# Cross attention's queries as seven block products per pair of heads, and the pooling mixer's bias and scale rows loaded ahead of its first sums

## The chip, the cores and the metric

The kernel runs on one core of one Trainium2 chip. Its engines, with the names that the profile uses: TensorE (PE for matmuls, PEld for loading their stationary operand), VectorE (DVE), ScalarE (ACT), GpSimd (POOL) and SyncE (SP), which here only issues transfers. The metric is the device time of one execution in microseconds, the median of several runs. Before the change it is 1936.6 us, from 1935.6 to 1938.74 over three runs.

## The reference

Two layers of a decoder trunk over 512 tokens of width 1024, in float32. Layer 0 mixes tokens by differential attention, layer 1 by a causal pooling mixer; both layers then attend to 256 memory tokens with 4 heads of 256, and a half-step SwiGLU feed-forward stands at either end of a layer.

```python
for i in range(DEPTH):
    x = layer_norm(a * x + 0.5 * swiglu_ffn(x, ffn_w_in[i, 0], ffn_w_out[i, 0]), ...)
    h = diff_attention(...) if i == 0 else pool_mixer(x, pool_w[j], pool_b[j], pool_scale[j])
    x = layer_norm(a * x + h, ...)
    x = layer_norm(a * x + memory_cross_attention(x, mem, xa_wq[i], xa_wkv[i], xa_wo[i]), ...)
    x = layer_norm(a * x + 0.5 * swiglu_ffn(x, ffn_w_in[i, 1], ffn_w_out[i, 1]), ...)

def pool_mixer(x, w_grp, b_grp, scale):
    ...
    pooled = jnp.stack(pooled, axis=2) - xg
    y = jnp.einsum('bsgc,gcd->bsgd', pooled, w_grp) + b_grp
    return y.reshape(B, S, D) * scale

def memory_cross_attention(x, mem, wq, wkv, wo):
    q = (x @ wq).reshape(B, S, XA_HEADS, XA_HEAD_DIM)
    k, v = jnp.split(mem @ wkv, 2, axis=-1)
    s = jnp.einsum('bshd,bmhd->bhsm', q, k) * (XA_HEAD_DIM ** -0.5)
    p = jax.nn.softmax(s, axis=-1)
    o = jnp.einsum('bhsm,bmhd->bshd', p, v).reshape(B, S, D_MODEL)
    return o @ wo
```

## The kernel before

**Numbers.** Every float32 operand of a matmul is split into a high part (ScalarE casts it to fp32r) and a low part (VectorE subtracts the high one from it): `split`, lines 120 and 121, or `split_scaled`, lines 125 and 126. Each product is then three matmuls, high by high, high by low and low by high (`mm3`, lines 205 to 207). So every weight tile costs one ScalarE cast and one VectorE subtraction before PE can use it.

**Stages.** The token rows lie in four tiles X, 128 tokens each. Each stage ends in sums that are added to X, followed token tile by token tile by the layer norm (`ln_token`, lines 366 to 380, with one small operation of GpSimd for the root), and the next stage's operands are the transposes of X (`turn`, tiles pt), split into xh and xl. The feed-forward already multiplies by seven block products instead of eight (`up`, `second_factors`, `seven`, `down`): both matrices are cut in two by two blocks, sums of blocks are made, and seven products of them are combined. It makes the sums of weight blocks by loading a further block onto the tile in place: a transfer from GpSimd's queue with an addition (line 666). `factors` 0 to 3 are the four blocks of the transposed X (0 and 1 for tokens 0 to 255, upper and lower half of the features; 2 and 3 for the other tokens, 3 being a difference), 4 to 6 sums of them.

**Cross attention.** `xa_main` is a generator that issues matmuls in program order, and `weave` lets a second generator, `xa_side`, take a step each time the first has issued a given number of estimated nanoseconds (2500 here). The main one makes, head by head, keys and values of the memory (`xa_k`, `xa_v`, banks pk and pv) and the head's queries (lines 1441 to 1452, banks xq): one transfer of 1 MB of `xa_wq`, two tiles of weights split, 16 groups of three matmuls of 512 tokens, and a scaled split of each of the two banks. The side steps of a head are its scores and softmax (banks xs, tiles p), the transposes of p, and the products with the values (banks xo), whose splits oT feed `to_tokens`, which multiplies by `xa_wo` and adds to X. In layer 1 the keys and values of heads 0 and 1 and the keys of head 2 are made ahead (`early_kv`), while the pooling mixer runs as its side.

**Pooling mixer.** X is split untransposed; for each of eight column blocks of 128, banks pp collect matmuls with a band matrix, and the block is split into a tile `pooled`. At block 2 (line 1261) `pool_weights` is issued: ScalarE scales the bias rows, GpSimd multiplies them by the scale rows, VectorE multiplies the mixer's weights pw by the scale rows (line 1239), and GpSimd adds the bias to X (line 1243). pw, the rows (tiles ps) and the norm's gains are loaded by `load_more`, which stands inside the first head's keys.

**Queues and tiles.** Each tile tag has a number of buffers; an instruction that writes a new tile waits until the buffer's last user is done, and a stage's tiles lie where those of the stage before lay. Every engine works through its instructions in an order that is fixed when the program is built; SP's transfers are issued in order, so one that waits for a buffer holds those behind it. Before, the stages around the change have five buffers each for the high and low weights (wh, wl) and two of 8 KB per partition for raw weights.

## Time and profile before

| | us |
|---|---|
| median of three runs | 1936.6 |
| the profiled execution | 1932.35 |
| its span, first to last instruction | 1930.6 |
| PE busy in it | 1902.1 |
| DVE busy in it | 1566.3 |
| ACT busy in it | 1022.2 |
| POOL busy in it | 315.0 |
| layer 0's cross attention, about | 591 to 736 |
| layer 1's pooling mixer with early keys and values, about | 1407 to 1464 |
| layer 1's cross attention, about | 1464 to 1597 |

All rows are of one profiled execution. A row of a timeline gives the start, the duration (of a merged group, to its end), engine, line and operation, what it writes and reads, and in square brackets how long the engine stood idle before it and what ended that. A row that groups gives count, total busy time, the mean of one in nanoseconds, and the idle time before. A row of stretches gives the busy time of each engine in it, and the granted clock of PE as a share of full speed. Matmuls are pipelined, so the time that one of them takes on PE is read from start to start and not from its duration.

### The profile page before, as it was taken

Reading aid. Unit: us, or ns where it says so; the run is one execution under the profiler, and the core shown is the slowest. Engines: PE = TensorE matmul, PEld = TensorE weight load, DVE = VectorE, ACT = ScalarE, POOL = GpSimd, SP = SyncE. Lnnn points to the kernel's source line nnn. Section 1 sums busy time; section 2 is a strip of 40 time slices with the busy share of each in tenths; the row PEclk is TensorE's granted clock in tenths of the full one; section 3 lists DMA queues with packets and bytes.
Section 4 is the critical chain, followed back from the end, with each engine's and each line's share of the span. In section 5 each row is a group of like instructions: output and inputs, shape, how many; then the busy total and the mean of one; then the engine's idle time right before and its main releaser. Section 6 shows DMA issues by size and latency. Waiting matters only on the chain.

```text
span 1930.6 us, 32520 instructions
## 1 busy us (share of the span) xinstructions
PE 1902.1 (99%) x13114; PEld 1740.5 (90%) x13114; DVE 1566.3 (81%) x2200; ACT 1022.2 (53%) x1580; POOL 315.0 (16%) x276
## 2 busy tenths in 40 slices
PE   8999999999999999999999999999999999999998
PEld 8999998888778888999998999999889889999997
DVE  7888889888867557888888988898887568988886
ACT  6555454567655435655554655455445436555553
POOL 2112121111210001211210321112040012111210
PEclk9999999999999999999999999999999999999999
DMA  9978772322134316977686587778244356867861
GB/s 239 220 169 182 175 138 77 90 80 74 48 117 142 110 66 186 186 175 164 139 194 179 104 179 168 177 162 185 89 153 134 115 140 120 181 158 170 183 133 56
DMA packets 246743, 277.96 MB, mean 144 GB/s; under 512 B 8256, under 2 KB 212544, under 8 KB 246592
## 3 DMA queue, kind: packets, MB, share of 16 engines
q0 software_dynamic: 92928, 92.29, 31.1%
q1 hardware_dynamic: 153664, 183.59, 29.2%
q8 instruction: 103, 1.69, 0.3%
q14 instruction: 48, 0.39, 0.1%
HBM read 273.75 MB, written 2.10 MB: 143 GB/s over the span
## 4 chain that ended last, share of the span: by engine, by line
PE 80%; DVE 12%; ACT 3%; DMA 2%; issue 2%; POOL 1%; SPq 1%; DVEq 0%; ACTq 0%; POOLq 0%
PE x L205 7%; PE x L206 7%; PE x L207 7%; PE z L206 4%; PE z L205 4%; PE z L207 4%; PE ps L205 4%; PE ps L207 4%; PE ps L206 4%; PE px L205 2%; PE px L207 2%; PE px L206 2%; DVE wl L121 2%; PE y L207 2%; PE x L681 2%
## 5 line engine op out<-in xcount | busy, mean ns | idle before, releaser
L666 POOL DMA_DIRECT2D ra<-in_ffn_w_in_dram x132 | 170.3, 1309 | 993.5 <-DVE wl L121 815.2
L120 ACT CAST wh<-ra 128x1024 fp32r<-128x1024 f32 x184 | 193.7, 1053 | 218.9 <-PE x L206 67.5
L121 DVE TENSOR_TENSOR wl<-ra,wh 128x1024 fp32r<-128x1024 f32 x184 | 223.8, 1220 | 73.0 <-ACT wh L120 72.5
L120 ACT CAST wh<-rc 128x1024 fp32r<-128x1024 f32 x136 | 143.1, 1053 | 118.6 <-PE x L206 43.1
L205 PE MATMUL x<-xe,wh 128*128 128x256 f32 x704 | 195.0, 277 | 0.0
L206 PE MATMUL x<-xe,wh 128*128 128x256 f32 x704 | 194.8, 277 | 0.0
L207 PE MATMUL x<-xe,wl 128*128 128x256 f32 x704 | 194.8, 277 | 0.0
L121 DVE TENSOR_TENSOR wl<-rc,wh 128x1024 fp32r<-128x1024 f32 x136 | 164.6, 1219 | 28.4 <-ACT wh L120 28.1
L120 ACT CAST wh<-b 128x1024 fp32r<-128x1024 f32 x112 | 117.8, 1052 | 131.3 <-PE x L206 67.7
L121 DVE TENSOR_TENSOR wl<-b,wh 128x1024 fp32r<-128x1024 f32 x112 | 136.7, 1220 | 40.2 <-ACT wh L120 40.2
L205 PE MATMUL x<-xh,wh 128*128 128x256 f32 x544 | 151.1, 278 | 0.0
L206 PE MATMUL x<-xl,wh 128*128 128x256 f32 x544 | 150.6, 277 | 0.0
L207 PE MATMUL x<-xh,wl 128*128 128x256 f32 x544 | 150.6, 277 | 0.0
L206 PEld LDWEIGHTS x<-xe,wh 128*128 128x128 f32 x704 | 132.5, 188 | 1.4
L205 PEld LDWEIGHTS x<-xe,wh 128*128 128x128 f32 x704 | 132.1, 188 | 1.3
L207 PEld LDWEIGHTS x<-xe,wl 128*128 128x128 f32 x704 | 132.2, 188 | 0.0
L121 DVE TENSOR_TENSOR wl<-raw,wh 128x1024 fp32r<-128x1024 f32 x64 | 81.8, 1285 | 38.8 <-ACT wh L120 38.2
L206 PEld LDWEIGHTS x<-xl,wh 128*128 128x128 f32 x544 | 102.5, 188 | 0.7
L205 PEld LDWEIGHTS x<-xh,wh 128*128 128x128 f32 x544 | 102.1, 188 | 0.7
L207 PEld LDWEIGHTS x<-xh,wl 128*128 128x128 f32 x544 | 102.1, 188 | 0.0
L207 PE MATMUL y<-xh,wl 128*128 128x256 f32 x352 | 98.4, 280 | 1.2
L206 PE MATMUL z<-xl,wh 128*128 128x256 f32 x352 | 97.5, 277 | 0.7 <-DVE xl L121 0.7
(429 smaller groups left out, 6291.6 us busy)
## 6 DMA issues: line engine op xcount, KB each, us to landing
ra<-in_ffn_w_in_dram POOLq DMA_DIRECT2D x132, 512.0 KB, 6.7
rc<-in_ffn_w_in_dram SPq DMA_DIRECT2D x88, 512.0 KB, 5.8
b<-in_ffn_w_out_dram SPq DMA_DIRECT2D x76, 512.0 KB, 4.8
ra<-in_ffn_w_in_dram SPq DMA_DIRECT2D x44, 512.0 KB, 5.4
rc<-in_ffn_w_in_dram POOLq DMA_DIRECT2D x44, 512.0 KB, 6.7
raw<-in_xa_wkv_dram SPq DMA_DIRECT2D x16, 1024.0 KB, 5.4
raw<-in_da_w_qkv_dram SPq DMA_DIRECT2D x16, 512.0 KB, 5.2
raw<-in_xa_wq_dram SPq DMA_DIRECT2D x8, 1024.0 KB, 4.9
```

What stands on the lines that cost most here:

```text
L120: self.nc.scalar.copy(hi, src),
L121: self.nc.vector.tensor_sub(lo, src, hi.bitcast(F32)),
L205: mm(out, w[0], x[0], start=start, stop=False, skip_group_check=again)
L206: mm(out, w[0], x[1], start=False, stop=False, skip_group_check=again)
L207: self.last_mm = mm(out, w[1], x[0], start=False, stop=stop, skip_group_check=again)
L666: nc.gpsimd.dma_start(t, source(*block), accum_op=ALU.add)
L681: self.last_mm = nc.tensor.matmul(ps[:, j], v[i][:, k, j * P : (j + 1) * P], x[l][:, k], start=n == i == l == 0, stop=n == 7 and i == 1, s ...
```

## The change

**Queries.** Two heads form a pair; the query weights of a pair are cut into four blocks of 512 rows by 256 columns (one column block for each head) and the transposed X into four of 512 features by 256 tokens. `xa_queries` makes seven products of 24 matmuls each. The weights' sums are made as in the feed-forward: one raw tile takes block (1, 1) and then three additions in place, another takes (2, 2) and one addition, each issued on GpSimd's queue behind the split of what stood in the tile. `xa_factors` makes the factors from the transposes of token tiles 2 and 3 (its parts are issued at each `s` of `XA_ORDER`), so `turn` serves only tiles 0 and 1. `XA_ORDER` writes out, for each layer, in what order the main work is issued: `q` and `r` are a product of the first and second pair, a digit is a part of that head's keys and values, `Q` and `R` hand the pair's heads to the side work.

**Buffers.** Raw weights come in pieces of 4 KB per partition, with five buffers in layer 0 and four in layer 1, and `to_tokens` takes its weights in the same pieces; wh and wl have four buffers instead of five. The side's step is 2100 instead of 2500.

**Pooling mixer.** The rows of scale and bias are no longer loaded in `load_more` but in `pool_bias`, which is issued right behind the first head's raw keys and values, into tiles p of the stage, and which also holds their two multiplications. `pool_weights` is issued at block 1 instead of 2. Behind the last token tile's sums no `turn` is issued.

```diff
+XA_ORDER = ("0000s00ss" "qq1q11qq1q11qQ" "r222r2r22rr3rrR33333", "qsqs2qsq2sq3qqQ" "r2r3rr33rrrR33")
...
+            ns = ns or 0
...
+    def raw_quarter(self, w, r0, c0, width):
+        raw = self.raw_tile((4 * 256 // width, width))
+        rows = w[r0 : r0 + P * 4 * 256 // width, c0 : c0 + width]
+        self.last_load = self.nc.sync.dma_start(raw, rows.rearrange("(k p) n -> p k n", p=P))
+        return raw
+    def raw_keys(self, w, h):
+        return [self.raw_quarter(w, 0, h * 256 + j * P, P) for j in range(2)]
+    def raw_values(self, w, h):
+        return [self.raw_quarter(w, r, D + h * 256, 256) for r in (0, S)]
...
-        for k in range(0, kn, 4):
-            n = min(4, kn - k)
-            raw = self.raw_tile((4, S))
+        got, n = [], self.raw_rows
+        for k in range(0, kn, n):
+            raw = self.raw_tile((n, S))
             r0 = (k0 + k) * P
             self.nc.sync.dma_start(
-                raw[:, :n], w[r0 : r0 + n * P, c0 : c0 + S].rearrange("(k p) n -> p k n", p=P)
+                raw, w[r0 : r0 + n * P, c0 : c0 + S].rearrange("(k p) n -> p k n", p=P)
             )
             if homes:
-                got += [home() for home in homes]
-                for j, t in enumerate(got):
+                got += [home() for home in homes[k : k + n]]
+                for j, t in enumerate(got[k:]):
                     self.split(t[0], t[1], raw[:, j])
...
-        if self.ln_next == "ffn":
+        if self.ln_next != "da":
...
+    def pool_bias(self):
+        nc = self.nc
         rows, self.pool_rows = self.a["pool_b"].rearrange("l g c -> l (g c)"), []
         for half in range(2):
             c = slice(half * S, (half + 1) * S)
-            sc, bs = self.tmp("ps"), self.tmp("ps")
+            sc, bs = self.tmp("p"), self.tmp("p")
             nc.sync.dma_start(sc, self.a["pool_scale"][:, c].to_broadcast([P, S]))
             nc.sync.dma_start(bs, rows[:, c].to_broadcast([P, S]))
+            nc.scalar.mul(bs, bs, 1.0 / ALPHA)
+            nc.gpsimd.tensor_tensor(bs, bs, sc, ALU.mult)
             self.pool_rows.append((sc, bs))
 
     def pool_weights(self):
 
         nc = self.nc
         for half, (sc, bs) in enumerate(self.pool_rows):
-            nc.scalar.mul(bs, bs, 1.0 / ALPHA)
-            nc.gpsimd.tensor_tensor(bs, bs, sc, ALU.mult)
...
-            if c == 2:
+            if c == 1:
...
-            self.turn_late()
+            if t < NT - 1:
+                self.turn_late()
...
-    def xa_kv(self, w, h):
-        kt = self.keys.pop(0) if self.keys else (yield from self.xa_k(w, h))
-        return kt, (yield from self.xa_v(w, h))
-    def xa_k(self, w, h, raw=None, then=None, turn=True):
-        rk = raw or self.raw_cols(w, h * 256)
+    def xa_kv(self, w, h, turn=None):
+        kt = self.keys.pop(0) if self.keys else None
+        if not kt:
+            kt = yield from self.xa_k(w, h, turn=turn)
+            yield None
+        self.kv.append((kt, (yield from self.xa_v(w, h))))
+    def xa_k(self, w, h, raw=None, then=None, turn=None):
+        rk = raw or self.raw_keys(w, h)
         ps = self.mm("pk").rearrange("p (c n) -> p c n", c=2)
         for j in range(2):
+            wk = self.hl([P, KC, P])
             with self.after(self.x_split if raw and not then else ()):
-                wk = self.cols(rk, j)
+                self.split_weights(wk[0], wk[1], rk[j])
             if then and j == 1:
                 then()
             for k in range(KC):
                 yield self.mm3(
                     ps[:, j], (wk[0][:, k], wk[1][:, k]), self.memT[k], k == 0, k == KC - 1
                 )
+            yield None
         kt = self.kv_tiles((P, 2, MEM))
         if turn:
-            self.turn_late()
+            turn()
         self.split(kt[0], kt[1], ps)
...
-            o = self.pair("oT")
-            self.split(o[0], o[1], po)
-            self.oT.append(o)
+            if c == 0:
+                o = self.pair("oT" if len(self.oT) < 4 else "xe", (P, 2, S))
+            self.split(o[0][:, c], o[1][:, c], po)
+            self.oT.append((o[0][:, c], o[1][:, c]))
...
+    def xa_factors(self):
+        nc, F, H = self.nc, self.factors, 2 * P
+        a11, a12, a21, s1 = (self.tmp("oT", (P, 4, H)) for i in range(4))
+        def part(i, x, o=slice(0, H)):
+            self.split(F[i][0][:, :, o], F[i][1][:, :, o], x)
+        for t in (2, 3):
+            o = slice(t % 2 * P, (t % 2 + 1) * P)
+            pts = []
+            for half in range(2):
+                pt = self.aux("pt", ("py", "yz")[half]).rearrange("p (c n) -> p c n", c=4)
+                c0 = half * S
+                with self.behind():
+                    self.transpose4(pt, [self.X[t][:, c0 + j * P : c0 + (j + 1) * P] for j in range(4)])
+                pts.append(pt)
+            nc.scalar.copy(a21[:, :, o], pts[0])
+            nc.vector.tensor_tensor(s1[:, :, o], pts[1], a21[:, :, o], ALU.subtract)
+            part(3, s1[:, :, o], o)
+            part(2, pts[1], o)
+            yield
+        for r, (hi, lo) in zip((a11, a12), F):
+            nc.vector.tensor_tensor(r, hi.bitcast(F32), lo.bitcast(F32), ALU.add)
+        s2, s4, s3 = s1, a12, a21
+        nc.vector.scalar_tensor_tensor(s2, s1, -1.0, a11, ALU.mult, ALU.subtract)
+        nc.vector.scalar_tensor_tensor(s4, s2, -1.0, a12, ALU.mult, ALU.subtract)
+        part(6, s4)
+        yield
+        part(4, s2)
+        nc.vector.tensor_tensor(s3, a11, a21, ALU.subtract)
+        part(5, s3)
+        yield
+    def xa_queries(self, w, h, q):
+        nc, H = self.nc, 2 * P
+        def source(row, col):
+            c0 = (h + col - 1) * H
+            return w[(row - 1) * S : row * S, c0 : c0 + H].rearrange("(k p) n -> p k n", p=P)
+        def load(*block):
+            t = self.raw_tile((4, H))
+            nc.sync.dma_start(t, source(*block))
+            return t
+        def more(t, *block):
+            nc.gpsimd.dma_start(t, source(*block), accum_op=ALU.add)
+        def operand(raw):
+            v = self.hl([P, 4, H])
+            self.split_weights(v[0], v[1], raw)
+            return v
+        def product(ps, v, a, start=False):
+            x = self.factors[a]
+            for j in range(2):
+                o = slice(j * P, (j + 1) * P)
+                for k in range(4):
+                    yield self.mm3(
+                        ps[:, j], (v[0][:, k, o], v[1][:, k, o]), (x[0][:, k], x[1][:, k]),
+                        start and j == k == 0, j == 1 and k == 3, True,
+                    )
+        bank = lambda t: t.rearrange("p (j n) -> p j n", j=2)
+        halves = slice(0, H), slice(H, S)
+        scale = (D // XA_H) ** -0.5
+        def done(i, half, src, by):
+            hi, lo = (t[:, :, halves[half]] for t in q[i])
+            self.split_scaled(hi, lo, src, by)
+        ra = load(1, 1)
+        x = bank(self.aux("x", "px"))
+        v = operand(ra)
+        more(ra, 1, 2)
+        rc = load(2, 1)
+        yield from product(x, v, 0, True)
+        p1 = self.tmp("p", (P, 2, H))
+        nc.scalar.copy(p1, x)
+        yield None
+        y = bank(self.aux("y", "yz"))
+        v = operand(rc)
+        yield from product(y, v, 1, True)
+        nc.vector.tensor_tensor(p1, y, p1, ALU.add)
+        q[0] = self.pair("q", (P, 2, S))
+        done(0, 0, p1, scale)
+        yield None
+        z = bank(self.aux("z", "yz"))
+        v = operand(ra)
+        rd = load(2, 2)
+        more(ra, 2, 2)
+        yield from product(z, v, 3, True)
+        p5 = self.tmp("p", (P, 2, H))
+        nc.scalar.copy(p5, z)
+        yield None
+        v = operand(rd)
+        more(rd, 1, 2)
+        yield from product(z, v, 6)
+        yield None
+        v = operand(ra)
+        more(ra, 2, 1)
+        yield from product(x, v, 4)
+        u2 = self.tmp("p", (P, 2, H))
+        q[1] = self.pair("q", (P, 2, S))
+        nc.scalar.copy(u2, x)
+        nc.vector.tensor_tensor(u2, z, u2, ALU.add)
+        done(1, 0, u2, -scale)
+        yield None
+        yield from product(x, operand(rd), 5)
+        nc.vector.tensor_tensor(p5, x, p5, ALU.add)
+        done(1, 1, p5, -scale)
+        yield None
+        yield from product(x, operand(ra), 2)
+        done(0, 1, x, scale)
+        yield None
+    def part(self, units):
+        for ns in units:
+            if ns is None:
+                return
+            yield ns
...
     def xa_main(self, layer):
         wq, wkv = self.a["xa_wq"][layer], self.a["xa_wkv"][layer]
-        early = len(self.kv)
-        for h in range(XA_H):
-            if h >= len(self.kv):
-                self.kv.append((yield from self.xa_kv(wkv, h)))
-            kt, v = self.kv[h]
-            raw = self.raw_cols(wq, h * 256)
-            qs = []
-            ws = [self.cols(raw, c) for c in range(2)]
-            ps = [self.mm("xq") for c in range(2)]
-            for p in ((0, 2 * P), (2 * P, S)) if self.late else ((0, S),):
-                for c in range(2):
-                    yield from self.project(ps[c], ws[c], (p,))
-                    self.turn_late(max(len(self.late) - 1, 0) if c == 0 else 0)
-            for c in range(2):
-                q = self.pair("q")
-                self.split_scaled(q[0], q[1], ps[c], (D // XA_H) ** -0.5)
-                qs.append(q)
-            self.heads.append((self.clock, (qs, kt, v)))
-            if 0 < early and h + early < XA_H:
-                self.kv.append((yield from self.xa_kv(wkv, h + early)))
+        self.late, second = [], self.xa_factors()
+        qs = [[None] * 2 for n in range(2)]
+        works = {n: self.xa_queries(wq, 2 * i, qs[i]) for i, n in enumerate("qr")}
+        works.update((str(h), self.xa_kv(wkv, h)) for h in range(1, XA_H))
+        works["0"] = self.xa_kv(wkv, 0, lambda: next(second))
+        for n in XA_ORDER[layer]:
+            if n == "s":
+                next(second)
+            elif n in "QR":
+                i = "QR".index(n)
+                for j in range(2):
+                    q = [(qs[i][j][0][:, c], qs[i][j][1][:, c]) for c in range(2)]
+                    self.heads.append((self.clock, 2 * i + j, q))
+            else:
+                yield from self.part(works[n])
         yield from self.to_tokens(self.oT, self.a["xa_wo"][layer], 0, 4, True, False, ALPHA)
 
     def xa_side(self):
         for h in range(XA_H):
-            while h >= len(self.heads) or self.clock < self.heads[h][0] + 3000:
+            while h >= min(len(self.heads), len(self.kv)) or self.clock < self.heads[h][0] + 3000:
                 yield WAIT
-            yield from self.xa_head(*self.heads[h][1])
+            yield from self.xa_head(self.heads[h][2], *self.kv[h])
...
-        bufs = dict(q=8, oT=10, gb=2)
+        bufs = dict(xe=6, q=4, oT=4)
+        self.raw_rows = 2
         if layer == 0:
             self.kv, self.keys = [], []
             mem = self.side_pool("mem")
-            with self.other_pools():
+            with self.stage_pools(4, dict(raw=5), ("wh", "wl", "raw", "kv")):
                 self.stage["mem"] = mem
-                with self.phase_pool(("gb", "gb"), "p", pT=6, p=4, kv=8, _x=0, **bufs):
-                    self.kvp = self.phase["kv"]
+                with self.phase_pool(("xe", "xe"), "p", p=4, pT=4, _x=0, **bufs):
+                    self.kvp = self.stage["kv"]
                     with self.tc.high_priority():
                         self.load_memory("p")
                     self.xa(layer, ln)
             self.close_side()
         else:
-            with self.later, self.phase_pool(("gb", "gb"), "p", _x=0, pT=6, p=4, **bufs):
+            with self.later, self.phase_pool(("xe", "xe"), "p", _x=0, pT=4, p=4, **bufs):
                 self.xa(layer, ln)
 
     def xa(self, layer, ln):
-        self.heads, self.oT = [], []
-        self.weave(self.xa_main(layer), self.xa_side(), 2500)
+        self.heads, self.oT, self.factors = [], [], self.factor_tiles()
+        self.weave(self.xa_main(layer), self.xa_side(), 2100)
...
-            self.later.enter_context(self.other_pools(("wh", "wl", "mem", "raw")))
+            self.later.enter_context(self.stage_pools(4, dict(raw=4), ("wh", "wl", "mem", "p", "raw")))
             self.to_w(self.later)
             self.kvp = self.later.enter_context(self.pool("kv"))
-            bufs = dict(pw=1, ps=4, gb=2, _x=0, pooled=16, sq=1)
+            bufs = dict(p=4, pw=1, gb=2, _x=0, pooled=16, sq=1)
             with self.phase_pool(("gb", "gb"), "sq", **bufs):
                 side = self.pool_mixer(layer, ln)
                 with self.tc.high_priority():
                     self.load_memory()
                 w = self.a["xa_wkv"][layer]
-                raws = [self.raw_cols(w, c) for c in (0, D)]
+                raws = [self.raw_keys(w, 0), self.raw_values(w, 0)]
+                self.pool_bias()
```

24 lines of the change are left out of this document (13 added, 11 removed).

## The prediction

> **What bounds the kernel now.** I read the page first, then busy time by stretch for both cross-attention stages and one stretch of feed-forward, then the timeline of each engine through the pooling mixer.
>
> ```profile
> span 1930.6 us, 32520 instructions
> PE 1902.1 (99%) x13114; PEld 1740.5 (90%) x13114; DVE 1566.3 (81%) x2200; ACT 1022.2 (53%) x1580; POOL 315.0 (16%) x276
> 591.00:736.00 145.00, 144.80 (x895) 128.27 (x894) 82.61 (x129) 59.58 (x113) 1.08 (x1) 1.00 0.37 119
> 1464.00:1597.00 133.00, 132.53 (x772) 115.12 (x769) 80.69 (x136) 56.48 (x112) 5.72 (x6) 1.00 0.45 135
> 800.00:1000.00 200.00, 199.71 (x1496) 188.81 (x1496) 176.59 (x223) 109.43 (x134) 36.04 (x28) 1.00 0.77 173
> ```
>
> The three stretches are layer 0's cross attention, layer 1's, and a stretch of feed-forward; the columns are busy time and instructions of PE, PEld, DVE, ACT and POOL, then the clock, the DMA share and GB/s. PE is the bound. In the two cross-attention stages it sits idle 0.2 and 0.5 us, while DVE is busy 82.6 of 145 us and 80.7 of 133. So a matmul taken out there shortens the run by its own spacing, as long as nothing else becomes late. The feed-forward row is what the new scheme looks like when it runs well: the same seven-product pattern, DVE at 176.6 of 200 us, PE idle 0.3.
>
> The one large hole that the change touches is in the pooling mixer:
>
> ```profile
> 1381.31 28.37 SPq L233 DMA_DIRECT2D raw<-in_xa_wkv_dram  x3
> 1412.65 8.90 DMA ps<-in_pool_b_dram
> 1421.57 0.63 ACT L1234 ACTIVATE ps<-ps 128x512 f32<-128x512 f32 x1 [1.89 <-DMA ps<-in_pool_b_dram]
> 1419.77 1.43 POOL L1235 TENSOR_TENSOR ps<-ps 128x512 f32<-128x512 f32 x1 [5.55 <-ACT ps L1234]
> 1421.28 3.77 POOL L1243 TENSOR_TENSOR X<-X,ps 128x512 f32<-128x512 f32 x3
> 1425.00 1.73 POOL L1235 TENSOR_TENSOR ps<-ps 128x512 f32<-128x512 f32 x1
> 1426.70 9.58 POOL L1243 TENSOR_TENSOR X<-X,ps 128x512 f32<-128x512 f32 x5
> 1422.71 0.69 DVE L121 TENSOR_TENSOR pooled<-pp,pooled 128x512 fp32r<-128x512 f32 x1 [2.66 <-ACT pooled L120]
> 1424.52 6.17 DVE L1239 TENSOR_TENSOR pw<-pw,ps 128x512 f32<-128x512 f32 x4
> 1437.42 0.58 PE L206 MATMUL ps<-wl,pooled 128*128 128x256 f32 x1 [3.11 <-DVE wl L121]
> 1437.79 0.41 PE L207 MATMUL ps<-wh,pooled 128*128 128x256 f32 x1
> ...
> 1440.57 0.41 PE L205 MATMUL pv<-wh,mem4h 128*128 128x256 f32 x1
> 1437.00:1439.00 2.00, 1.58 (x7) 1.58 (x8) 2.00 (x3) 0.00 (x0) 0.00 (x0) 0.61 1.07 376
> 1439.00:1441.00 2.00, 2.00 (x12) 2.00 (x11) 2.00 (x4) 0.00 (x0) 0.00 (x0) 0.53 0.16 51
> ```
>
> The last bias row is issued at 1412.65 and takes 8.9 us. ACT waits for it (1421.57), and behind ACT's multiplication stands its cast of the first pooled block, so DVE idles 2.66 us until 1422.71. DVE then needs 6.17 us for four weight multiplications, 1.54 us each, against 0.68 us for other 512-column operations of this engine (below). The split of those weights comes late and PE waits 3.11 us. After it PE runs at a granted clock of 0.61 and 0.53: the 13 steps from 1437.79 to 1440.57 are 0.214 us each instead of 0.118, some 16 matmuls losing 1.6 us together. Hole and slow stretch are 4.7 us.
>
> **Products.** Per layer the queries are 3 x 64 matmuls of 512 columns. The change makes them two pairs of heads, seven products each, 24 matmuls of 256 columns per product: 336 of 256.
>
> ```profile
> L205 PE MATMUL xq<-xh,wh 128*128 128x512 f32 x64 | 25.8, 404 | 0.0
> 662.25 0.39 PE L206 MATMUL xq<-xl,wh 128*128 128x512 f32 x1
> ...
> 664.58 0.39 PE L207 MATMUL xq<-xh,wl 128*128 128x512 f32 x1
> 647.68 0.28 PE L207 MATMUL pk<-mem0h,wl 128*128 128x256 f32 x1
> ...
> 658.22 0.28 PE L207 MATMUL pv<-wh,mem6l 128*128 128x256 f32 x1
> 815.06 2.72 PE x L681 x24
> 1080.80 2.83 PE x L681 x24
> ```
>
> Start to start, 10 steps of 512 columns take 2.33 us (0.233 each), 93 steps of 256 take 10.54 us (0.113); whole products take 2.72 or 2.83 us (0.113 or 0.118). Now: 192 x 0.233 = 44.7 us. After: 336 x 0.113 = 38.1, or 336 x 0.118 = 39.6. The gain is 5.1 to 6.6 us a layer; should the 512-column spacing be 0.229 where the stage is calmer, 4.3. I take 5.5, so **11.0 us for two layers** (8.6 to 13.2). Transposes stay as many as before.
>
> **What the products add beside PE.** Weight splits go from 8 to 14 a layer, factors 4 to 6 and their sums are new, and the outputs are put together from three adds and four scaled lows per pair.
>
> ```profile
> L121 DVE TENSOR_TENSOR wl<-raw,wh x26: 1214/1225/1227, 594.4 to 694.4; 128x1024 fp32r<-128x1024 f32 x26
> L120 ACT CAST wh<-raw x24: 1043/1052/1067, 601.2 to 693.3; 128x1024 fp32r<-128x1024 f32 x24
> L126 DVE SCALAR_TENSOR_TENSOR q<-xq,q 128x512 fp32r<-128x512 f32 x8 | 5.5, 683 | 0.1
> L611 DVE TENSOR_TENSOR hb<-xh,xl 128x1024 f32<-128x1024 f32 x2 | 2.4, 1214 | 0.0
> L631 DVE TENSOR_TENSOR hb<-pt,hb 128x512 f32<-128x512 f32 x2 | 1.4, 680 | 0.0
> L637 DVE SCALAR_TENSOR_TENSOR sr<-hb 128x1024 f32<-128x1024 f32 x1 | 1.2, 1211 | 0.0
> ```
>
> DVE: 6 splits x 1.22 = 7.3; factor arithmetic as the feed-forward has it, two sums 2.4, two differences 1.4, three more of 1.2, so 7.4; three whole-factor splits 3.7; outputs 14 x 0.68 instead of 8, so 4.1. Together 22.5 us a layer, which makes layer 0's stage 105 of about 139 us, 76%, under the 88% that the feed-forward carries. ACT gains less (6 x 1.05, three copies of products a pair, three factor casts: about 14 us on 60). On average this is hidden by PE; if the cover went, DVE's 22.5 us would stand bare. It is the order that can hurt, at three places.
>
> First, layer 1's factor 6. The last token is transposed when its norm is done, product 3 follows, and product 4 needs factor 6.
>
> ```profile
> 1467.90 1.06 PE L489 MATMUL pt<-ident,X 128*128 128x128 f32 x8 [0.47 <-DVE X L380]
> 765.05 1.04 PE L489 MATMUL pt<-ident,X 128*128 128x128 f32 x8
> 775.77 1.21 DVE L121 TENSOR_TENSOR xe<-hb,xe 128x1024 fp32r<-128x1024 f32 x1
> ```
>
> Today PE already waits 0.47 us for that norm. In the feed-forward the way from the transposes to a split factor 6 takes 11.9 us (765.05 to 776.98), about 5.7 of it other DVE work. In cross attention the other work in that place is one product's add and low (1.4) and two weight lows (2.4): some 10 us. The cover is one half of head 2's values, product 3, and the other half if it is drawn ahead: 3 x 2.75 = 8.3. I take **2 us** lost (0, if only the chain's own 6.3 counts, to 6.4, if one half stays behind). In layer 0 four blocks lie between, so nothing.
>
> Second, the accumulating loads. One tile carries W11, then three additions in place through POOL's queue, and each addition must wait for the split of the sum before it, behind which the next split waits.
>
> ```profile
> L666 POOL DMA_DIRECT2D ra<-in_ffn_w_in_dram x132: 1273/1282/1785, 11.1 to 1857.2; - x132
> DMA to landing us min/median/max: 5.6/6.7/14.8
> ```
>
> A link is a split (1.05 and 1.22 in a row), 6.7 us to landing, and about 0.6 for hand-overs: 9.6. Three links are 28.8 us. The first pair has six products and four key or value halves beside them in layer 0 (10 x 2.75 = 27.5), three in layer 1 (24.8); the first split runs a few us ahead. I take 1 us each, **2 us** (0 to 8, if one of the six lands at the maximum). The second pairs have two heads' scores beside them and are covered. POOL's own time, ten issues of 1.3 us a layer, falls where it is idle (1.08 us busy in layer 0's row); SP's queue has the same bytes in smaller pieces.
>
> Third, the last two steps of head 3 in layer 1: heads start in pairs, and at 2100 ns a step about ten of the twelve steps fit beside what is left of the main work. **1 us** (0 to 3).
>
> **Pool rows.** They are issued behind four weight pieces that all have a buffer, so near 1381 where the first raw load now goes out, not at 1412; at 8.9 us they land by about 1395, and ACT (53% busy over the span) and POOL multiply them there. The multiplications of the pooling weights go one block earlier. DVE's 2.66 us hole closes and POOL's 3.2 us of multiplications leave the crowded stretch, which is more than PE's 3.11 us wait; without the wait the slow clock stays away too. I take **4 us** of the 4.7 (at best 4.9, with the small waits around it; at worst a loss of 3.2, if both multiplications delay the norms that the last sums feed). Four split buffers instead of five cost nothing by the feed-forward row, which lives with four.
>
> [...]
>
> **Sum** on the profiled execution, 1932.35 us around its span of 1930.6: -11.0 - 4.0 + 2.0 + 2.0 + 1.0 = -10.0, so 1922.3. The median of the runs, 1936.6, lies 4.25 above this execution; on its scale the forecast is **1926.6**.
>
> **Rivals.** (A) *The accumulating chain binds.* If an addition lands after about 10 us instead of 6.7, a pair's links are 38.7 us against covers of 27.5 and 24.8; with 5 us of lead the two first pairs lose 15 us, and with the other terms (-15 + 3 + 15) the kernel ends 3 us up, 1939.6. It decides the sign when the pairs lose over 12 us. For it: one landing of 14.8. Against: the median, and a DMA share of 0.37 here to 0.77 in the feed-forward. (B) *DVE's burst eats the gain.* Factor 6 costs 6.4 in layer 1 and its successors (factors 4 and 5, 1.2 us each behind two splits) as much again, and the late values push the heads: 8 more lost, 1934.6, no change. For it: DVE is busy 2.00 of 2.00 us in both rows around the slow clock. Against: the feed-forward's 88%. (C) *The change does not do what it says for the rows*: the two POOL multiplications hold up the norms by 3.2, or the hole only moves; then the pool term is -0.8, and the time 1929.8.
>
> **How the numbers follow.** Forecast 0.55 (its own range 1920 to 1931), C 0.17, B 0.10, A and any like it 0.18. About 0.2% (3.9 us) is what a measurement of this kernel can tell from no change. Faster: forecast and C, 0.72. Same: B, 0.10. Slower: 0.18. The range goes from the best ends (-13.2 - 4.9, so 1918.5) to A at 1939.6 rounded up: 1918 to 1940.
>
> **What would show it.** Query matmuls: 336 of 256 columns a layer at 0.113 to 0.118. Right if PE's idle time from 1410 to 1445 falls from over 3.1 to under 1 us, no stretch there has a clock under 0.9, and DVE's multiplications of the pooling weights start by about 1420. The link is read from the issues of accumulating loads on the query weights: near 6.7 us, with the wait of products 3, 5 and 7 for their splits under 1 us. Factor 6 is read at product 4 of layer 1's first pair. Wrong would be PE idle over 12 us in the two stages together, or waits for split weights in the second pairs, which I call covered.

## The result, and the profile after

| | before | after |
|---|---|---|
| median of the runs, us | 1936.6 (1935.6 to 1938.7) | 1951.4 (1950.6 to 1953.0) |
| ratio to before | | 1.0080, 95% interval 1.0065 to 1.0094 |
| span of the profiled execution, us | 1930.6 | 1948.7 |

The kernel became 0.8% slower. The forecast was 1926.6 us, with a chance of 0.18 for slower and a range up to 1940; the time lies above that too.

The page after begins as follows; PE's share fell by one point, though it has 240 matmuls more.

```profile
span 1948.7 us, 33225 instructions
PE 1903.5 (98%) x13354; PEld 1754.1 (90%) x13354; DVE 1606.2 (82%) x2244; ACT 1047.6 (54%) x1614; POOL 340.0 (17%) x292
```

To see where the 18.1 us of span went, I cut both executions at the same places of PE's timeline: the first key matmul of layer 0's cross attention, the last matmul that sums its output, the first key matmul beside the pooling mixer, the first query matmul of layer 1, and the last output sum of layer 1. First the kernel before, then the one after; the first column is the start.

```profile
591.27 0.36 PE L205 MATMUL pk<-mem0h,wh 128*128 128x256 f32 x1
754.67 0.40 PE L207 MATMUL ps<-kv,oT 128*128 128x512 f32 x1
1407.51 0.28 PE L205 MATMUL pk<-mem0h,wh 128*128 128x256 f32 x1
1464.55 0.28 PE L205 MATMUL xq<-xh,wh 128*128 128x256 f32 x1
1599.55 0.40 PE L207 MATMUL ps<-kv,oT 128*128 128x512 f32 x1
```

```profile
591.52 0.36 PE L208 MATMUL pk<-mem0h,wh 128*128 128x256 f32 x1
765.66 0.40 PE L210 MATMUL ps<-kv,xe 128*128 128x512 f32 x1
1419.43 0.28 PE L208 MATMUL pk<-mem0h,wh 128*128 128x256 f32 x1
1470.77 0.28 PE L208 MATMUL x<-xh,wh 128*128 128x256 f32 x1
1614.68 0.40 PE L210 MATMUL ps<-kv,xe 128*128 128x512 f32 x1
```

| stretch, us | before | after | difference |
|---|---|---|---|
| layer 0's cross attention | 163.4 | 174.1 | +10.7 |
| from there to the pooling mixer's keys | 652.8 | 653.8 | +0.9 |
| pooling mixer | 57.0 | 51.3 | -5.7 |
| layer 1's cross attention | 135.0 | 143.9 | +8.9 |
| from there to the end | 331.0 | 334.0 | +2.9 |

The pooling mixer gained what was hoped for and somewhat more. Both cross attentions, which were to gain 5.5 us each, lost. Between the profiled executions below, a stretch whose code is the same differs by up to 1.3 us in layer 1 and 1.9 in layer 0, so one difference of that size carries no argument by itself. The waits of PE, first from 590 to 760 us, then from 1455 to 1620 (line, what it waited for, us in total, times, longest), and a table by stretch (busy time and instructions of PE, PEld, DVE, ACT, POOL, then clock, DMA share, GB/s):

```profile
PE x L208 <- ACT p L1572: 5.7, 1, 5.7
PE y L210 <- DVE wl L124: 3.6, 1, 3.6
PE pt L1433 <- DVE p L1425: 1.2, 1, 1.2
```

```profile
PE pt L506 <- DVE xl L124: 5.2, 1, 5.2
PE pk L208 <- ACT wh L123: 1.6, 1, 1.6
```

```profile
600.00:620.00 20.00, 16.39 (x119) 16.19 (x118) 19.39 (x23) 11.24 (x15) 1.70 (x2) 0.83 0.43 106
640.00:660.00 20.00, 19.58 (x149) 19.58 (x150) 12.48 (x17) 10.12 (x16) 1.28 (x1) 0.86 0.64 158
1480.00:1500.00 20.00, 13.12 (x82) 12.41 (x83) 17.11 (x19) 9.69 (x13) 3.90 (x3) 0.80 0.52 101
```

Three single waits carry most of the loss, all in the first pair of a layer, and the clock is low after each (0.83, 0.86 and 0.80). They have two makers. Products are named here by their factor, 0 to 6; a pair issues them in the order 0, 1, 3, 6, 4, 5, 2, and the prediction counts them in that order.

**The first wait is DVE's order.** The timeline of DVE and of PE in layer 0:

```profile
607.52 1.21 DVE L1489 SCALAR_TENSOR_TENSOR oT<-oT 128x1024 f32<-128x1024 f32 x1
608.66 1.22 DVE L1494 TENSOR_TENSOR oT<-oT 128x1024 f32<-128x1024 f32 x1
609.79 1.21 DVE L1490 SCALAR_TENSOR_TENSOR oT<-oT 128x1024 f32<-128x1024 f32 x1
610.93 2.35 DVE L124 TENSOR_TENSOR wl<-raw,wh 128x1024 fp32r<-128x1024 f32 x2
612.20 0.58 PE L210 MATMUL y<-xh,wl 128*128 128x256 f32 x1 [3.61 <-DVE wl L124]
616.85 0.41 PE L210 MATMUL y<-xh,wl 128*128 128x256 f32 x1
```

Three operations for factors 4, 5 and 6, which PE needs only for its fourth product and later, stand ahead of the split that PE needs now, for the second product. And that product's 22 matmuls that follow take 0.221 us each ((616.85 - 612.20)/21) instead of 0.113.

**The second and third are a cast that waits for an addition,** with other work behind it. ACT, DVE, POOL and PE in layer 0, then layer 1:

```profile
606.67 1.05 ACT L123 CAST wh<-raw 128x1024 fp32r<-128x1024 f32 x1 [0.33 <-DMA raw<-in_xa_wq_dram]
617.91 1.22 DVE L124 TENSOR_TENSOR wl<-raw,wh 128x1024 fp32r<-128x1024 f32 x1
619.66 1.28 POOL L1514 DMA_DIRECT2D raw<-in_xa_wq_dram  x1 [17.46 <-DVE wl L124]
626.71 2.94 ACT L123 CAST wh<-raw 128x1024 fp32r<-128x1024 f32 x3 [3.34 <-DMA raw<-in_xa_wq_dram]
629.46 1.29 POOL L1514 DMA_DIRECT2D raw<-in_xa_wq_dram  x1 [5.66 <-DVE wl L124]
638.84 1.04 ACT L123 CAST wh<-raw 128x1024 fp32r<-128x1024 f32 x1 [7.75 <-DMA raw<-in_xa_wq_dram]
639.79 0.58 ACT L1572 COPY p<-x 128x512 f32<-128x512 f32 x1
640.42 0.58 PE L208 MATMUL x<-xe,wh 128*128 128x256 f32 x1 [5.67 <-ACT p L1572]
```

```profile
1471.99 1.31 POOL L1514 DMA_DIRECT2D raw<-in_xa_wq_dram  x1 [2.95 <-DVE wl L251]
1481.24 1.04 ACT L123 CAST wh<-raw 128x1024 fp32r<-128x1024 f32 x1 [5.54 <-DMA raw<-in_xa_wq_dram]
1482.19 0.61 ACT L123 CAST xh<-oT 128x512 fp32r<-128x512 f32 x1
1482.83 0.69 DVE L124 TENSOR_TENSOR xl<-oT,xh 128x512 fp32r<-128x512 f32 x1 [5.28 <-ACT xh L123]
1484.27 1.08 PE L506 MATMUL pt<-ident,X 128*128 128x128 f32 x4 [5.25 <-DVE xl L124]
```

In layer 0 the first sum is cast at 606.67, as soon as its addition, issued at 600.84, has landed. The low part of that sum comes only at 617.91: on DVE it stands behind the factors' arithmetic and splits and behind the sum that waits for the late second product. The second addition overwrites the tile that this split reads, so it goes out at 619.66. From there the chain runs on: the second sum is cast at 626.71, the tile's third addition goes out at 629.46 (the fourth of the pair, as one to the other tile lies between), and its sum is cast 9.4 us later. Product 5, for which PE waits 5.67 us, does not need that sum; it needs the bank that the copy at 639.79 frees, and the copy stands on ACT behind the cast. In layer 1 the same kind of cast stands on ACT ahead of the casts of the second tokens' factors, so DVE, and behind it PE's transposes, wait for a transfer that they do not need.

**The pooling mixer** gained as forecast. SP, POOL and DVE there, then the only waits of PE from 1419 to 1471, then the stretch of the pooling weights:

```profile
1376.43 0.42 SPq L1246 DMA_DIRECT2D p<-in_pool_scale_dram  x1
1388.27 0.41 SPq L1247 DMA_DIRECT2D p<-in_pool_b_dram  x1
1395.17 1.29 POOL L1249 TENSOR_TENSOR p<-p 128x512 f32<-128x512 f32 x1 [0.69 <-ACT p L1248]
1439.36 2.49 DVE L1259 TENSOR_TENSOR pw<-pw,p 128x512 f32<-128x512 f32 x4
```

```profile
PE pk L210 <- DVE wl L124: 1.1, 3, 0.5
```

```profile
1430.00:1440.00 10.00, 9.83 (x86) 9.63 (x85) 8.98 (x10) 6.50 (x10) 3.84 (x2) 1.00 0.92 300
```

The rows are issued by 1388, both products are done by 1396.5, PE's wait of 3.1 us and the slow clock are gone (1.00 here). DVE's four multiplications of the pooling weights, 6.17 us before beside POOL's additions, take 2.49 us behind them (the last two end at 1435.8).

### The profile page after: what moved, and what is told of

Read it like the earlier page. It is cut to its first block, busy times and chain, and to the rows that moved or that the text cites. A ratio compares the mean times of both kernels' runs of the same rounds, so it can differ in the third digit from the quotient of the medians.

```text
span 1948.7 us, 33225 instructions
## 1 busy us (share of the span) xinstructions
PE 1903.5 (98%) x13354; PEld 1754.1 (90%) x13354; DVE 1606.2 (82%) x2244; ACT 1047.6 (54%) x1614; POOL 340.0 (17%) x292
## 4 chain that ended last, share of the span: by engine, by line
PE 75%; DVE 14%; ACT 4%; DMA 3%; issue 2%; POOL 1%; SPq 0%; DVEq 0%; ACTq 0%; POOLq 0%
PE x L208 7%; PE x L209 7%; PE x L210 7%; PE z L210 4%; PE z L209 4%; PE z L208 4%; PE ps L208 4%; PE ps L210 4%; PE ps L209 4%; DVE wl L124 3%; PE px L210 2%; PE px L208 2%; PE px L209 2%; DMA raw<-in_xa_wq_dram 2%; PE y L210 2%
## 5 line engine op out<-in xcount | busy, mean ns | idle before, releaser
L208 PE MATMUL x<-xe,wh 128*128 128x256 f32 x768 | 214.5, 279 | 6.3 <-ACT p L1572 5.7
L210 PE MATMUL x<-xe,wl 128*128 128x256 f32 x768 | 213.7, 278 | 0.7 <-DVE wl L124 0.7
L209 PE MATMUL x<-xe,wh 128*128 128x256 f32 x768 | 213.7, 278 | 0.0
L208 PE MATMUL x<-xh,wh 128*128 128x256 f32 x608 | 169.0, 278 | 0.0
L210 PE MATMUL x<-xh,wl 128*128 128x256 f32 x608 | 168.3, 277 | 0.5 <-DVE wl L251 0.5
L209 PE MATMUL x<-xl,wh 128*128 128x256 f32 x608 | 168.4, 277 | 0.0
L208 PEld LDWEIGHTS x<-xe,wh 128*128 128x128 f32 x768 | 145.3, 189 | 8.3 <-ACT p L1572 6.2
L209 PEld LDWEIGHTS x<-xe,wh 128*128 128x128 f32 x768 | 145.7, 190 | 1.4
L210 PEld LDWEIGHTS x<-xe,wl 128*128 128x128 f32 x768 | 145.4, 189 | 0.9 <-DVE wl L124 0.9
L124 DVE TENSOR_TENSOR wl<-raw,wh 128x1024 fp32r<-128x1024 f32 x76 | 98.6, 1303 | 29.6 <-ACT wh L123 29.0
L209 PEld LDWEIGHTS x<-xl,wh 128*128 128x128 f32 x608 | 114.5, 188 | 0.7
L123 ACT CAST wh<-raw 128x1024 fp32r<-128x1024 f32 x76 | 78.8, 1048 | 57.2 <-DMA raw<-in_xa_wq_dram 25.0
```

Source lines behind the costliest of these rows:

```text
L123: self.nc.scalar.copy(hi, src),
L124: self.nc.vector.tensor_sub(lo, src, hi.bitcast(F32)),
L208: mm(out, w[0], x[0], start=start, stop=False, skip_group_check=again)
L209: mm(out, w[0], x[1], start=False, stop=False, skip_group_check=again)
L210: self.last_mm = mm(out, w[1], x[0], start=False, stop=stop, skip_group_check=again)
```

## The experiments

Each ratio below is to the kernel before, run on the same chip beside it; the kernel after stands at 1.0080. At the end of the section the stretches of the runs stand in one table.

**The rows' part alone, in the kernel before.**

```diff
+    def pool_bias(self):
...
             nc.sync.dma_start(bs, rows[:, c].to_broadcast([P, S]))
+            nc.scalar.mul(bs, bs, 1.0 / ALPHA)
+            nc.gpsimd.tensor_tensor(bs, bs, sc, ALU.mult)
...
-            if c == 2:
+            if c == 1:
...
                 raws = [self.raw_cols(w, c) for c in (0, D)]
+                self.pool_bias()
```

> The kernel before, with the rows' part alone: rows issued behind the first raw loads, multiplied there, weights multiplied one block earlier. The queries stay three passes of 512 columns. Theory (the rows' part works and all of the loss sits in cross attention): the stretch from the first pooling keys to the queries, 57.0 us before and 50.5 us after, shortens by 5 to 6 us here too, so 1930 to 1932 us. Rival (the gain of that stretch came from the one turn of 0.8 us moved out of it and from other changes of the layout): 1935 to 1937 us.

Measured 1938.6 us, ratio 1.0034 (1.0014 to 1.0054): slower, outside both ranges, and the stretch grew from 57.0 to 59.5 us. Its SP, POOL, DVE and PE:

```profile
1407.37 0.34 SPq L1230 DMA_DIRECT2D ps<-in_pool_scale_dram  x1
1414.54 4.65 POOL L1247 TENSOR_TENSOR X<-X,ps 128x512 f32<-128x512 f32 x3
1420.38 0.55 POOL L376 TENSOR_TENSOR rstd<-var,mhalf 128x1 f32<-128x1 f32 x1
1420.96 2.27 DVE L380 SCALAR_TENSOR_TENSOR X<-X,rstd,sr 128x1024 f32<-128x1024 f32 x1 [5.41 <-POOL rstd L376]
1423.94 0.33 PE L1278 MATMUL pp<-bandh,xh 128*128 128x128 f32 x1 [4.25 <-ACT xh L120]
```

Here the rows are issued only at 1407, not at 1376. POOL then has its multiplications and additions ahead of the last norm's power, DVE waits 5.41 us for it and PE 4.25. That is the mechanism of the forecast's rival C (priced at 3.2 us), and it came true where the rows stay late. So this run does not separate the rows' part from the new buffers; the next does.

**The rows' part undone, in the kernel after** (loads behind the pooling weights, multiplications with them, one block later).

```diff
         nc.sync.dma_start(self.pool_w, w.rearrange("(k p) n -> p k n", p=P))
+        self.pool_bias()
...
-            nc.scalar.mul(bs, bs, 1.0 / ALPHA)
-            nc.gpsimd.tensor_tensor(bs, bs, sc, ALU.mult)
             self.pool_rows.append((sc, bs))
...
         for half, (sc, bs) in enumerate(self.pool_rows):
+            nc.scalar.mul(bs, bs, 1.0 / ALPHA)
+            nc.gpsimd.tensor_tensor(bs, bs, sc, ALU.mult)
...
-            if c == 1:
+            if c == 2:
...
-                self.pool_bias()
                 next(side)
```

> The changed kernel with the rows' part alone undone: rows load behind the pooling weights, are multiplied with the weights, and these go one block later, all in the new buffers. Theory (the stretch from the first pooling keys to the queries went from 57.0 to 51.3 us through the rows' part): 1951.4 + 5.5 = 1957 us, 1954 to 1959. Rival (it went through the smaller pieces of the key and value loads and the last turn moved out; with the rows alone in the old buffers the stretch was 59.5 us): 1949 to 1953 us.

Measured 1956.5 us, ratio 1.0104 (1.0089 to 1.0119), and 55.5 us for the stretch: in the new buffers the rows' part is worth 4.1 us of stretch (55.5 - 51.3).

**No additions:** their transfers are left out, so the sums are not made.

```diff
         def more(t, *block):
-            nc.gpsimd.dma_start(t, source(*block), accum_op=ALU.add)
+            return
```

> The changed kernel without its accumulating loads: each sum of weight blocks is left at its first block, so products 3, 4, 5 and 2 use W11 or W22 alone and the output is another one; products, splits and order of the program stay. Theory of the late additions (they landed 9.2 and 9.4 us after their issue where the two long waits of 5.67 and 5.25 us end): both waits and the slow clock behind them (2.4 and 1.7 us) and layer 1's waits of 2.6 us go, 1951.4 - 17 = 1934 us, 1931 to 1938; layer 0's wait of 3.6 us for a weight split stays. Rival (the order of the casts and of the factor arithmetic alone makes the loss): over 1946 us.

Measured 1936.0 us, ratio 1.0001 (0.9991 to 1.0010), as the theory of the late additions said. The waits of 5.67 and 5.25 us are gone, that of 3.61 us in layer 0 stays, and in layer 1 PE now waits 3.1 us for a factor cast. The run takes the traffic of the additions away together with the waits for them, and does not separate the two.

**One order on ACT in layer 1:** the cast for product 3 behind the casts of the factors (`last_part` is the last split of factor 2).

```diff
         z = bank(self.aux("z", "yz"))
-        v = operand(ra)
+        with self.after(self.last_part):
+            v = operand(ra)
```

> The changed kernel with one order on ACT: the cast of the sum for product 3 stands behind the casts of the second tokens' factors, in layer 1; loads and additions as they are. Theory of the queue (in layer 1 a cast that waits for an addition holds up the factor casts, the transposes behind them and so PE): the wait of 5.25 us and the slow clock of 1.7 us behind it go, at most 1.5 us of wait for the sum itself takes their place, 1951.4 - 5.5 = 1946 us, 1944 to 1947. Rival (the addition's landing at 1481.2 us is what binds, whatever stands behind the cast): the wait moves to product 3's split, 1949 to 1952 us.

Measured 1951.4 us, ratio 1.0081 (1.0066 to 1.0096): no gain, the theory of the queue by itself fails. PE's largest wait in layer 1, and ACT's row for it:

```profile
PE pk L208 <- ACT wh L123: 5.5, 1, 5.5
```

```profile
1495.36 1.99 ACT L123 CAST wh<-raw 128x1024 fp32r<-128x1024 f32 x2 [2.74 <-DMA raw<-in_xa_wq_dram]
```

The transposes no longer wait, but the next cast that waits for an addition stands ahead of a key block's cast, and PE loses 5.46 us there. The place of the wait is a matter of order; that there is one is a matter of the chain.

**The factors later in layer 0.**

```diff
-XA_ORDER = ("0000s00ss" "qq1q11qq1q11qQ"
+XA_ORDER = ("0000s00" "qqs1q1s1qq1q11qQ"
```

> The changed kernel with the sums and splits of factors 4 to 6 of layer 0 put behind the first two products instead of ahead of them (another order string, nothing else). Theory of DVE's burst (3.6 us of factor arithmetic stand ahead of the split for the second product, which waits 3.61 us, and 22 matmuls behind it run at 0.221 us): wait and slow clock, 6.0 us, go and the chain of additions starts earlier: 1943 to 1946 us. Rival (product 6 then waits for factor 6, or the next addition binds in its place): 1949 to 1953 us.

Measured 1939.7 us, ratio 1.0027 (1.0017 to 1.0037): 0.53% under the kernel after, 10.3 us, where 5 to 8 were expected. Layer 0's cross attention falls from 174.1 to 162.7 us. Besides the 3.61 us and the slow clock, the additions start earlier: the second goes out at 615.2 instead of 619.7, the fourth at 623.9 instead of 629.5, and the wait of 5.67 us at product 5 is gone; the largest left there is one of 2.06 us at product 4, for the cast of its own sum (shown in the last section).

**The factors later, and no additions.**

> The kernel with the factors later in layer 0 (1939.7 us), and the accumulating loads left out, so products 3, 4, 5 and 2 use single blocks and the output is another one. Theory (burst in layer 0 and additions in both layers are separate causes whose sum is the loss; what stays is layer 1's factor 6, 4.5 us of waits and 2.3 us of slow clock): 1936.0 - 6 = 1930 us, 1928 to 1932. Rival (one cause alone, the additions' chain started late by the burst: without additions the order is worth nothing): 1935 to 1937 us.

Measured 1931.3 us, ratio 0.9975 (0.9965 to 0.9985). Layer 0's cross attention takes 157.9 us: 5.5 less than before, which is the forecast's saving of the products; that it agrees to a tenth is luck. What layer 1 still loses, in this kernel's waits and its first stretch there:

```profile
PE z L208 <- ACT xe L123: 3.1, 1, 3.1
PE z L209 <- DVE xe L124: 1.0, 1, 1.0
```

```profile
1455.00:1475.00 20.00, 17.35 (x147) 16.82 (x146) 20.00 (x24) 12.82 (x21) 0.62 (x1) 1.00 0.30 89
```

DVE is busy for the whole of these 20 us, and PE waits for factor 6, first for its high part and then for its low part.

**As that, and in layer 1 without factors 4 to 6.**

```diff
+        if self.ln_layer:
+            F[4:7] = F[0], F[1], F[3]
+            yield
+            yield
+            return
         for r, (hi, lo) in zip((a11, a12), F):
```

> The kernel with factors later in layer 0 and no additions (1931.3 us), and in layer 1 without the arithmetic and splits of factors 4 to 6: products 6, 4 and 5 take factors 3, 0 and 1, and the output is another one. Theory (DVE's burst makes what layer 1 loses without additions, 6.2 us of waits on its factor casts and lows and 2.4 us of slow clock): from the first query matmul to the last output sum 138.5 us fall to about 131, so 1931.3 - 7.5 = 1924 us, 1922 to 1926. Rival (other splits queue there, four weight buffers and layer 1's norms): 1928 to 1932 us.

Measured 1924.6 us, ratio 0.9951 (0.9935 to 0.9966); layer 1's cross attention falls from 138.5 to 131.9 us, and no wait for a factor is left. The arithmetic and splits of three factors cost layer 1 6.6 us.

**Three tries to relieve the chain of additions,** each on top of the factors later in layer 0: the two sums of the first factors on POOL, the first block loaded twice, head 1's blocks spread singly between the products.

```diff
-            nc.vector.tensor_tensor(r, hi.bitcast(F32), lo.bitcast(F32), ALU.add)
+            nc.gpsimd.tensor_tensor(r, hi.bitcast(F32), lo.bitcast(F32), ALU.add)
...
-        ra = load(1, 1)
+        r1, ra = load(1, 1), load(1, 1)
+        more(ra, 1, 2)
...
-XA_ORDER = ("0000s00" "qqs1q1s1qq1q11qQ"
+XA_ORDER = ("0000s00" "qqs1q1s1q1q1qq1Q"
```

> The kernel with the factors later in layer 0 (1939.7 us), and the two sums of the first factors, 1.21 us each a layer, on POOL instead of DVE. Theory (in layer 1 the additions' landing binds: transposes wait 3.6 us, a key block 2.5 us, both behind casts that wait for an addition): 1938 to 1941 us, no gain. Rival (DVE's burst, 20.0 of 20 us busy in layer 1's first stretch without the additions, binds): 1935 to 1937 us.

> The kernel with the factors later in layer 0 (1939.7 us), and the first block W11 loaded twice a pair: once for product 0, once as the tile that the additions go into, so that the first addition waits for its own load and not for the split of product 0. One load of 512 KB more a pair. Theory (in layer 1 the first addition, issued only after that split and 9.2 us in landing, makes the first wait): the 3.6 us and the slow clock of 1.7 us go, 1939.7 - 5 = 1935 us, 1933 to 1937. Rival (the second tile takes a raw buffer from the key and value pieces, or the next addition takes the wait over): 1939 to 1944 us.

> The kernel with the factors later in layer 0 (1939.7 us) and the same spread of head 1's blocks in layer 0; layer 1 has its seven products. Theory of cover: 1939.7 - 3 = 1936.5 us, 1935 to 1938. Rival (the wait moves to product 2): 1939 to 1941 us.

Measured 1950.5 us (ratio 1.0076, 1.0061 to 1.0091), 1940.0 (1.0022, 1.0012 to 1.0031) and 1945.4 (1.0055, 1.0042 to 1.0069). The first and the third lie outside both of their ranges. With the sums on POOL, layer 0 has waits of 4.8 and 2.7 us: beside the two sums, a weight split on DVE takes 3.42 and 4.08 us instead of 1.22 (by the pages the run's 76 such splits take 104.0 us, the kernel after's 98.6), and the first addition, which waits for such a split, goes out at 605.4 instead of 601.0. The second copy takes the 3.6 us of transposes down to 1.3, and a wait of 1.9 us for the add behind product 5 comes up. The spread moves layer 0's wait to product 2, as its rival said (2.6 and 1.0 us there), but at a higher price than the rival's.

**Plain queries in layer 1,** with the factors later in layer 0; then the same with the spread. `xa_plain` is the loop of the kernel before over the heads, with two loads of 128 columns a head and the new tiles.

```diff
     def xa_main(self, layer):
         wq, wkv = self.a["xa_wq"][layer], self.a["xa_wkv"][layer]
+        if layer:
+            yield from self.xa_plain(wq, wkv)
+            yield from self.to_tokens(self.oT, self.a["xa_wo"][layer], 0, 4, True, False, ALPHA)
+            return
...
-        self.weave(self.xa_main(layer), self.xa_side(), 2100)
+        self.weave(self.xa_main(layer), self.xa_side(), (2100, 2500)[layer])
```

> The kernel with the factors later in layer 0 (1939.7 us), whose layer 1 takes its queries as before in 64 matmuls of 512 columns a head and pass, with heads woven in as before; buffers, pieces and the rows' part stay as changed. Theory (all that layer 1 loses beside the forecast is in its seven products: from its first query matmul to the end 466.1 us before, 477.8 us with the change): 1939.7 - 11 = 1929 us, 1927 to 1931, 0.3 to 0.4% under the kernel before. Rival (the smaller buffers of layer 1, four weight splits instead of five and smaller raw tiles, cost it too): 1932 to 1938 us.

> As the kernel with plain queries in layer 1, and in layer 0 the key and value blocks of head 1 spread singly between products 3, 6, 4 and 5 (another order string). Theory (product 4 waits 2.06 us for the sum whose addition is issued behind product 3's split, with some 1.6 us of slow clock behind it; one block more between them covers the landing): 3 us under the kernel with plain queries, 1926 us, 1924 to 1928. Rival (the wait moves to product 2, which then stands right behind product 5): the same time as it within 1.5 us.

Measured 1932.3 us (ratio 0.9988, 0.9979 to 0.9997) and 1936.7 (1.0012, 1.0003 to 1.0021). Plain queries bring layer 1's cross attention to 136.9 us, 1.9 above before: the time lies 3 us above the theory's, so part of the rival holds. Of the 1.9 us, 0.8 is the turn that moved there from the pooling mixer; which buffer costs the rest was not tried. The spread loses here too.

**The first products amid head 0's blocks,** with plain queries in layer 1: six blocks instead of four lie between the pair's products. The two kernels differ in where product 3 stands.

```diff
-XA_ORDER = ("0000s00" "qqs1q1s1qq1q11qQ"
+XA_ORDER = ("000qsq000qs1qs1q11q1q1Q"
...
+XA_ORDER = ("000qsq0q00s1qs1q11q1q1Q"
```

> The kernel with plain queries in layer 1 (1932.3 us); in layer 0 products 0 and 1 run amid head 0's blocks, so that six blocks instead of four lie between the pair's products. Theory of cover (the additions cost layer 0 another 4.9 us because too little work lies between the products that wait for them): 4 us less, 1928 us, 1926 to 1930. Rival (the products then meet the last norms and the transposes on DVE, and product 3 waits instead): 1931 to 1936 us.

> As the kernel with products 0 and 1 amid head 0's blocks, product 3 one block earlier, so that its addition has 2.75 us less and product 4's 2.75 us more. Theory of cover: within 2 us of that kernel, above it if the first addition binds, under it if the second does. Rival (the cover does not matter): both within 0.5 us of 1932 us.

Measured 1936.5 us (ratio 1.0004, 0.9996 to 1.0013) and 1932.0 (0.9983, 0.9974 to 0.9992). With product 3 late, layer 0 still has a wait of 4.5 us; with product 3 one block earlier the largest is 2.0 us, and the time is 4.4 us less, more than the 2 us expected at most; it is 0.17% under before. Against the plain kernel with four blocks (1932.3 us) the six blocks gain nothing that can be told from noise. So more cover by itself did not help, and where it lies mattered: behind the second addition rather than the first.

| kernel, us | layer 0's cross attention | pooling mixer | layer 1's cross attention |
|---|---|---|---|
| before | 163.4 | 57.0 | 135.0 |
| after | 174.1 | 51.3 | 143.9 |
| no additions | 163.2 | 51.2 | 139.6 |
| factors later in layer 0 | 162.7 | 51.2 | 143.3 |
| both of these | 157.9 | 51.2 | 138.5 |
| and no factors 4 to 6 in layer 1 | 158.1 | 51.2 | 131.9 |
| factors later, plain layer 1 | 162.6 | 51.3 | 136.9 |
| amid head 0, product 3 early | 161.5 | 51.2 | 136.9 |

## Why the prediction was wrong

**Products, -11.0.** Right in size: -5.5 in layer 0 (157.9 against 163.4), and in layer 1 -3.9 once the additions and the factors are out of the way (131.9 against 135.0, with one turn of 0.8 us that moved there from the pooling mixer). The sum of 9.4 lies in the forecast's 8.6 to 13.2.

**Pool rows, -4.0.** Right: -4.1. Of the stretch's 5.7 us another 0.8 is the turn that moved out of it. One sign that I had named did not come: DVE's multiplications of the pooling weights start at 1439.4, not by 1420. That is 14.8 us later than before; 11.9 had been lost ahead, and the other 2.9, which bring them behind POOL's last additions, are not explained. The loss named as the worst end, 3.2 us through held-up norms, was seen where the rows load late (DVE's wait of 5.41 us for POOL); in the kernel after it did not come, PE's waits from 1419 to 1471 are 1.1 us together.

**"In layer 0 four blocks lie between, so nothing."** This step failed. I asked whether factor 6 would be ready in time, and it was. I did not ask what its arithmetic stands ahead of: a split for the second product, 3.6 us late, with 2.4 us of slow clock behind it (22 x (0.221 - 0.113)). Without the additions this order costs 5.4 us (163.2 against 157.9).

**Additions, +2.0 (0 to 8).** Mis-sized: with the factors later they cost 4.8 us in layer 0 (162.7 against 157.9), and in layer 1 they cost 4.3 (143.9 against 139.6). The transfer was sized well: the 16 additions land 5.7 to 9.3 us after their issue, 6.1 in the median, against 6.7. What failed is the link and its cover. The sum of three links against the sum of a pair's cover, 28.8 against 27.5, was the wrong question. A link's cover is only what lies between its own two products, and the next link does not start when the former addition has landed but when both parts of that sum are split, which on DVE happens in its order: in layer 0 the first addition went out at 600.84, the second at 619.66, 18.8 us for a link of 9.6; the next link took 9.8. And the forecast looked only at the products that need a sum, while the waits of 5.67 and 5.25 us fell on work that needs none and stands on ACT behind the cast. What four split buffers instead of five cost was not run by itself.

**Burst and additions compound.** In layer 0 they cost 16.3 us together (174.1 against 157.9), 6.1 more than 5.4 and 4.8. The same burst that delays the second product stands on DVE ahead of the chain's own split at 617.91; with the factors later the second addition goes out 4.5 us earlier. The forecast had priced A (additions, 1939.6) and B (burst, 1934.6) as rivals, of which one at most would come. Both mechanisms came, A's by the late start of its links and not by the slow landing that it named, and B's also in layer 0, where nothing was priced.

**Layer 1's factor 6, +2.0 (0 to 6.4).** Mis-sized: 6.6 for the arithmetic and splits of factors 4 to 6 together, a little over the upper bound, which had left out the slow clock (0.91 from 1475 to 1495 in the kernel with the factors later and no additions).

**Right besides:** the second pairs are covered (one wait of 1.2 us in layer 0); single products without a wait run at the spacing that was read from the feed-forward (0.113 us a matmul from 625.30 to 627.90, 0.118 from 1503.02 to 1505.61). The end's +1.0 can't be told: 2.9 us were lost behind layer 1's cross attention, 1.0 of them in one wait for the feed-forward's first splits, and the rest stays open.

## What to carry to other kernels

Where an engine takes its work in program order, as ACT did here (a factor's cast at 1482.19 only behind a cast that had waited 5.54 us), a chain's cover is counted link by link, from what lets its next step start, a place in an engine's queue too, and not as one sum against another. When work is added to an engine that is busy 57% on average, as DVE was in layer 0's cross attention, ask of each added operation what will stand behind it and who waits for that. Mechanisms priced as rivals may come together; where one delays what the other waits for, their costs add up to more than their sum.

## What the runs showed of the hardware

A gap of 2.06 us was followed by the slow clock. PE in the kernel with the factors later, around its largest wait in layer 0's cross attention:

```profile
622.25 0.39 PE L208 MATMUL x<-xe,wh 128*128 128x256 f32 x1 [2.06 <-ACT wh L123]
622.94 0.41 PE L210 MATMUL z<-xe,wl 128*128 128x256 f32 x1
626.13 0.38 PE L210 MATMUL z<-xe,wl 128*128 128x256 f32 x1
626.35 0.29 PE L208 MATMUL z<-xe,wh 128*128 128x256 f32 x1
```

PE resumes at full speed, drops to half at 622.94 and is back at 626.35, after 3.41 us: 16 matmuls at 0.213 us instead of 0.113, 1.6 us lost behind a wait of 2.06. The slow stretches behind the waits of 3.61 and 5.67 us in the kernel after, some 5.5 and 4.7 us long, begin as PE resumes. The length of a gap alone does not tell whether a slow stretch follows: with product 3's cast behind those of the factors, the second product's wait is again 3.61 us, and the 20 steps from 615.27 to 617.53 take 0.113 us each; amid head 0 with product 3 early, behind a wait of 2.04 us, the 20 from 637.25 to 639.52 take 0.114.
